# Regrouped score blocks, scaled queries and a two-part value product in a one-layer attention trunk

## The chip, the cores and the metric

The kernel runs on one core of a Trainium2 chip. The metric is the device time of one execution in microseconds (us). Five engines run side by side, each with an instruction queue of its own that it works off in order: TensorE (PE in the profile; PEld is its weight load), VectorE (DVE), ScalarE (ACT), GpSimd (POOL) and SyncE (SP, which here only issues transfers). TensorE writes to PSUM, eight banks of 512 fp32 columns; VectorE and ScalarE read it; GpSimd works in SBUF only.

## The reference, cut to what matters

One layer, 512 tokens, width 2048, sliding-window attention of 32 query heads (head dimension 64) over 4 key heads, a sink per head, a bias by distance, then a gated output product and a second gated block with an embedding. Everything is fp32.

```python
hn = x * rsqrt(mean(x*x) + eps) * norm_g
q, k, v, gate = split(hn @ w_in)                 # 2048, 256, 256, 2048 columns
scores = q.k / 8 + bias[distance]                # only 0 <= distance < 128
probs = exp(scores - m) / (sum(exp(scores - m)) + exp(sink - m))
x = x + ((probs @ v) * silu(gate)) @ w_out
g = sigmoid(rmsnorm(x) @ ple_gate)
out = rmsnorm(x + (p @ ple_proj) * g) * final_g
```

## The kernel before, in words

**Numbers.** fp32 operands are split into two rounded parts, high and low: ScalarE copies the high part (a CAST), VectorE subtracts it from the source to get the low part. A product is three matmuls (`mm3`, L117 to L122): high by high, low by high, high by low. A weight chunk of 128 x 1024 is loaded by SyncE (`Weights.load`, L99), split by ScalarE (`whi`, L106) and VectorE (`wlo`, L107), and used by eight steps of three 512-column matmuls. `Weights.get` splits two chunks ahead.

**First stage (L184 to L246).** For each of 16 slices k of the width: load a slice of x (transposed, with the norm's gain) and 768 columns of weights, split both, and multiply into PSUM: two banks of queries (`qps`, 6 matmuls of 512 columns), two of keys (`ktps`, 6 of 512), and four of values (`vps`, one per 128 tokens, 12 matmuls of 256 columns, half of each bank). Before it, 34 small matmuls (`warm_ps`, L136) run while the first loads land. The row norm 1 / rms (`rstd1`) is worked out from x on the side; it is a column per 128 tokens, and four transposes at the end of the stage (L249) and two copies (L251) spread it over the partitions as `rb`.

**Seam (L253 to L310).** `evac_q` splits a query bank into a tile of 8 groups of 64 queries, two heads side by side; keys and values are multiplied by 1 / rms, keys are laid out per key head (`make_key`), values are split (`V`), and GpSimd builds the differences of neighbouring value blocks (`diffs`, L333 and L334). The queries stay undivided; the score addition does that with `sclq`. GpSimd builds the table of the bias by distance (L299 to L310) and sends it to DRAM (`tdram`); SyncE reads back a skewed copy per pair of head pairs (`load_bias`, L359).

**Attention (L311 to L478).** 64 units: 8 sets `d` of four heads by 8 groups `g` of 64 queries. Unit i does `scores(i)`, then `turn(i-2)` and `weigh(i-3)` ahead of it, and between them seven steps (21 matmuls of 512 columns) of the projections of queries and gates, taken from a generator (`proj`). `scores` does two matmuls (L376), one per head pair, with 128 rows = 2 heads x 64 queries, over 128 keys (first two groups) or 192 keys, high and low part of the keys side by side: 256 or 384 columns. One two-bank tile takes them (`s`, one buffer: the next unit's matmuls wait until VectorE has read it). VectorE adds bias and both parts (L385 twice, with `sclq` as a per-row factor), folds the ends together (L400, since 192 keys hold 128 in the window), reduces the maximum (L402); ScalarE takes the exponential (L405); VectorE the reciprocal (L406); ScalarE scales (L408). `turn` transposes the result (L418) and splits it (L420, L421); `weigh` multiplies by V.

**Order.** The order on TensorE and SyncE is that of the program, on GpSimd too in the attention stage; the order on VectorE and ScalarE in the seam and the attention stage is set when the program is built, by a scheduler that sorts by expected readiness. [...]

**End.** After two Strassen-like products (L480 to L940) the last block of 128 rows is done in halves (`block`, L992); then a chain of one-column operations gives the last row norm (L1072 to L1077), and the four quarter rows are scaled (L1082, L906, L1083) and stored, two from SyncE's queue and two from ScalarE's (L901).

Of the kernel before, what the change touches and what calls it, by code (L numbers as in the profile page):

```python
# [11 lines left out]
F32 = mybir.dt.float32  # L12
F32R = mybir.dt.float32r
AF = mybir.ActivationFunctionType
ALU = mybir.AluOpType
# [4 lines left out]
S = 512  # L20
# [10 lines left out]
UNITS = S // HB  # L31
BUCKETS = 32
# [6 lines left out]
WARM = 34  # L39
PAD = 104  # L40
# [13 lines left out]
def trunk_kernel(ctx: ExitStack, tc: tile.TileContext, a: dict):  # L54
# [62 lines left out]
    def mm3(ps, sh, sl, mh, ml, first, last, more=False):  # L117


        nc.tensor.matmul(ps, sh, mh, start=first, stop=False, skip_group_check=more)  # L120
        nc.tensor.matmul(ps, sh, ml, start=False, stop=False, skip_group_check=more)  # L121
        nc.tensor.matmul(ps, sl, mh, start=False, stop=last, skip_group_check=more)  # L122


    sinkb = const.tile([P, PAIRS], F32, name="sinkb")
# [6 lines left out]
    ones = const.tile([P, P], mybir.dt.bfloat16, name="ones")  # L132
    nc.vector.memset(ones, 1.0)
# [10 lines left out]
    sclq = const.tile([P, UNITS], F32, name="sclq")  # L144
# [41 lines left out]
    for k in range(KC):  # L186
        wh = start_pool.tile([P, 768], F32R, tag="w0h", name=f"w0h{k}")
        wl = start_pool.tile([P, 768], F32R, tag="w0l", name=f"w0l{k}", bufs=2)
# [4 lines left out]
        cuts = [slice(512, 768), slice(0, 512)] if k == 0 else [slice(0, 768)]  # L193
        for c in cuts:
            nc.sync.dma_start(w0[:, c], a["w_first"][k][:, c])
# [10 lines left out]
        for c in cuts[-1:]:  # L206
            nc.scalar.copy(wh[:, c], w0[:, c])
            nc.vector.tensor_sub(wl[:, c], w0[:, c], wh[:, c].bitcast(F32))
# [4 lines left out]
        if f:  # L213
            for n, (sw, mx) in enumerate(((wh, h), (wl, h), (wh, l))):
                for t in range(2):
                    nc.tensor.matmul(q_ps[t], sw[:, qc[t]], mx, start=n == 0, stop=False)
        else:
            for t in range(2):
                mm3(q_ps[t], wh[:, qc[t]], wl[:, qc[t]], h, l, f, e)
# [11 lines left out]
        if k == 9:  # L231
            run(rsqrt_mean(rstd1, ssq1, D, "r1"))
            for e in range(2):
                for b in range(2):
                    nc.vector.tensor_scalar_mul(
                        sclq[HB * e : HB * e + HB].rearrange("p (n b) -> p n b", b=2)[:, :, b],
                        rstd1[HB * b : HB * b + HB], HD ** -0.5,
                    )
        if k == 10:
            for e in range(2):  # L240
                nc.sync.dma_start(sinkb[HB * e : HB * e + HB], a["sinks"][e].partition_broadcast(HB))
            nc.sync.dma_start(pn, a["ple_norm"])
        if k == 12:
            misc = quarter("misc")
            rcol = misc[:, 0].rearrange("p (t c) -> p t c", t=NB)
            nc.vector.tensor_copy(rcol, rstd1.unsqueeze(2).to_broadcast([P, NB, P]))  # L246
    W.load(3)
    for t in range(NB):
        nc.tensor.transpose(v_ps[t // 2][:, 256 + (t % 2) * P : 384 + (t % 2) * P], rcol[:, t, :], ident)  # L249
    for t in range(2):  # L250
        nc.vector.tensor_copy(rb[:, t * 256 : (t + 1) * 256], v_ps[t][:, 256:])  # L251
# [3 lines left out]
    def evac_q(c, ps):  # L255

        q = Q[c] = kvq.tile([P, UNITS, 2, HB], F32R, tag="q", name=f"q{c}", bufs=4)
        halves = slice(0, 64), slice(64, 128)
        for e in range(2):
            src = ps[halves[e]].rearrange("p (g q) -> p g q", q=HB)  # L260
            hi, lo = q[halves[e], :, e], q[halves[1 - e], :, e]
            nc.scalar.copy(hi, src)
            nc.vector.tensor_sub(lo, src, hi.bitcast(F32))

    for c in range(2):
        evac_q(c, q_ps[c])
# [26 lines left out]
    for t in range(NB):  # L293
        nc.vector.tensor_scalar_mul(heads(values[t]), heads(v_ps[t][:, :256]), rstd1[:, t : t + 1])
    split(V[0], values[0])


    relb, tvec = misc[:HEADS, 1, :BUCKETS], misc[:HEADS, 2, :TOEP]
# [25 lines left out]
    DV = apool.tile([P, NB - 1, 2, KVH * 2 * HD], F32R, name="DV")  # L324
    diffs = {}
# [26 lines left out]
    def load_bias(d):  # L352
        biases[d] = apool.tile([P, 2, P + HB], F32, tag="bias", name=f"bias{d}", bufs=2)
        for e in range(2):
            src = bass.AP(
                tensor=tdram.tensor, offset=tdram.offset + (4 * d + e) * TOEP + HB,
                ap=[[1, HB], [2 * TOEP, 2], [1, P + HB]],
            )
            nc.sync.dma_start(biases[d][HB * e : HB * e + HB], src)  # L359

    def scores(i):

        d, g = divmod(i, UNITS)
        odd = g % 2
        if g == 4 and d + 1 < TWOS:
            load_bias(d + 1)
        key = K[d // 2]

        first = max(g - 2, 0) * HB
        n = P if g < 2 else P + HB
        s_ps = spsum.tile([P, 2, S], F32, tag="w", name=f"s{i}")
        for u in range(2):
            st = Q[2 * d + u][:, g].rearrange("p e q -> p (e q)")
            nc.tensor.matmul(s_ps[:, u, : 2 * n], st, key[:, :, first : first + n], start=True, stop=True)  # L376
        t = apool.tile([P, 2, 4 + P + HB], F32, tag="t", name=f"t{i}", bufs=4)
        seen = t[:, :, 65:194] if odd else t[:, :, 0:129]
        pr = t[:, :, 65:193] if odd else t[:, :, 1:129]
        sink = 193 if odd else 0  # L380
        nc.gpsimd.tensor_copy(t[:, :, sink], sinkb[:, 2 * d : 2 * d + 2])
        bias = biases[d][:, :, ::-1]

        def add(out, in0, in1):
            nc.vector.scalar_tensor_tensor(  # L385
                out=out, in0=in0, scalar=sclq[:, g : g + 1], in1=in1, op0=ALU.mult, op1=ALU.add
            )

        if g < 2:
            if g == 0:  # L390
                nc.gpsimd.memset(t[:, :, 65:129], MASKED)
            n = HB * (g + 1)
            out = pr[:, :, :n]
            add(out, s_ps[:, :, :n], bias[:, :, 192 - n :])
            add(out, s_ps[:, :, P : P + n], out)
# [6 lines left out]
        nc.vector.tensor_reduce(sm[:, 0:2], seen, axis=AX.X, op=ALU.max, negate=True)  # L402
        for u in range(2):
            su = seen[:, u, :]
            nc.scalar.activation(su, su, AF.Exp, bias=sm[:, u : u + 1], accum_out=sm[:, 2 + u : 3 + u])  # L405
        nc.vector.reciprocal(sm[:, 4:6], sm[:, 2:4])  # L406
        for u in range(2):
            nc.scalar.mul(pr[:, u], pr[:, u], sm[:, 4 + u : 5 + u])  # L408
        T[i] = pr

    def turn(i):
# [8 lines left out]
        nc.scalar.copy(r[:, 0], pt)  # L420
        nc.vector.tensor_sub(r[:, 1], pt, r[:, 0].bitcast(F32))  # L421
# [635 lines left out]
    base, ms, rt, im, nw, yn = (const.tile([P, 1], F32, name=f"{v}_3") for v in ("base", "ms", "rt", "im", "nw", "yn"))  # L1057
# [4 lines left out]
    last = block(1, 1, "s", "o", slice(256, 512))()  # L1062
    next(last)
    run(g)
    n = done[3]
    nc.vector.tensor_reduce(base, ssq3[:, 3, : n - 1], axis=AX.X, op=ALU.add)
    nc.vector.tensor_scalar(base, base, 1.0 / D, EPS, op0=ALU.mult, op1=ALU.add)
    next(last)
# [8 lines left out]
    nc.vector.scalar_tensor_tensor(out=yn, in0=rt, scalar=im, in1=nw, op0=ALU.mult, op1=ALU.mult)  # L1077
    for j, h in ((0, 2), (1, 3)):
        if j:
            row(3, j, yn)  # L1080
        else:
            nc.vector.tensor_scalar_mul(x1[j][:, 3, :], x1[j][:, 3, :], yn)  # L1082
        nc.scalar.mul(x1[h][:, 3, :], x1[h][:, 3, :], yn)  # L1083
        store(3, j)
        store(3, h, nc.scalar)


def laid_out(i):
# [24 lines left out]
        "sinks": f(np.asarray(i["swa_sinks"])[0].reshape(PAIRS, 2).T),  # L1113
# [19 lines left out]
```

## Time and profile before

| | us |
|---|---|
| median of 3 runs (lowest, highest) | 804.79 (804.75, 805.07) |
| the profiled execution | 804.96 |
| its span, first to last instruction | 803.0 |
| TensorE busy in the span | 792.2 (99%) |
| VectorE, ScalarE, GpSimd busy | 593.0, 500.8, 111.5 |

How to read it: rows of a timeline give the start from the beginning of the span, the duration, the engine and the line, the tiles (output <- inputs), the shape and a count; a bracket at the end is idle time before the row and what ended it. Matmuls overlap, so a matmul's price is the distance from its start to the next one's, not its duration. In groups by line, the two numbers after the bar are total busy us and mean ns of one.

### The profile page before, as it was taken

What the parts mean: (1) busy time and instruction counts of PE and PEld (TensorE: products, weight loads), DVE (VectorE), ACT (ScalarE), POOL (GpSimd) and SP (SyncE); (2) the same over time, 40 slices, a digit from 0 to 9 for tenths busy, and PEclk for the clock granted to TensorE, in tenths of its full rate; (3) what the DMA queues carried; (4) which work ended last, traced back from release to release, by engine and by line L of the source; (5) the groups of instructions that cost most, each with busy time, mean ns of one, the idle gap of its engine ahead of it and who ended that gap; (6) DMA issues with size and microseconds to landing.
All of it is one profiled execution on the core that took longest, in us unless ns stands there. A gap on an engine that the chain in (4) does not pass through costs nothing.

```text
span 803.0 us, 11080 instructions
## 1 busy us (share of the span) xinstructions
PE 792.2 (99%) x3828; PEld 664.9 (83%) x3828; DVE 593.0 (74%) x967; ACT 500.8 (62%) x1038; POOL 111.5 (14%) x216
## 2 busy tenths in 40 slices
PE   9999999999999999999999999999999999999995
PEld 8888888888888888888888888888888888888884
DVE  4547786887777777777778898766646656989896
ACT  5645466676667666675666655555568656657755
POOL 0101113122121313112122200030000020210000
PEclk9999999999999999999999999999999999999998
DMA  8862587778697877868694469998512996785533
GB/s 300 312 199 94 161 266 208 224 198 237 149 249 209 206 224 194 224 172 233 169 233 122 115 213 362 322 286 243 198 53 82 373 210 200 162 227 177 194 106 105
DMA packets 45144, 164.91 MB, mean 205 GB/s; under 512 B 5904, under 2 KB 8080, under 8 KB 41248
## 3 DMA queue, kind: packets, MB, share of 16 engines
q1 hardware_dynamic: 38080, 130.07, 47.9%
q0 software_dynamic: 6720, 33.61, 22.6%
q8 instruction: 30, 0.49, 0.2%
q10 hardware_dynamic: 288, 0.52, 0.2%
q14 instruction: 26, 0.21, 0.1%
HBM read 158.36 MB, written 46.19 MB: 255 GB/s over the span
## 4 chain that ended last, share of the span: by engine, by line
PE 96%; issue 1%; DVE 1%; ACT 0%; POOL 0%; ACTq 0%; DVEq 0%; POOLq 0%
PE gps L121 7%; PE gps L122 7%; PE gps L120 7%; PE qps L121 7%; PE qps L122 7%; PE qps L120 7%; PE o L121 6%; PE o L122 6%; PE o L120 6%; PE g L122 5%; PE g L121 5%; PE g L120 5%; PE s L376 2%; PE o L454 2%; PE pt L418 2%
## 5 line engine op out<-in xcount | busy, mean ns | idle before, releaser
L563 DVE TENSOR_TENSOR blo<-braw,bhi 128x1024 fp32r<-128x1024 f32 x80 | 97.6, 1223 | 38.5 <-ACT bhi L562 38.5
L562 ACT CAST bhi<-braw 128x1024 fp32r<-128x1024 f32 x80 | 84.0, 1051 | 65.2 <-PE g L122 19.2
L122 PE MATMUL gps<-xh,wlo 128*128 128x512 f32 x256 | 100.2, 391 | 0.0
L121 PE MATMUL gps<-xl,whi 128*128 128x512 f32 x256 | 100.2, 391 | 0.0
L120 PE MATMUL gps<-xh,whi 128*128 128x512 f32 x256 | 99.9, 390 | 0.0
L107 DVE TENSOR_TENSOR wlo<-wraw,whi 128x1024 fp32r<-128x1024 f32 x60 | 73.3, 1222 | 23.0 <-ACT whi L106 20.5
L122 PE MATMUL qps<-xh,wlo 128*128 128x512 f32 x224 | 87.8, 392 | 0.0
L120 PE MATMUL o<-bhi,fho 128*128 128x512 f32 x224 | 87.7, 392 | 0.0
L121 PE MATMUL qps<-xl,whi 128*128 128x512 f32 x224 | 87.7, 391 | 0.0
L121 PE MATMUL o<-blo,fho 128*128 128x512 f32 x224 | 87.3, 390 | 0.0
L122 PE MATMUL o<-bhi,flo 128*128 128x512 f32 x224 | 87.2, 389 | 0.0
L120 PE MATMUL qps<-xh,whi 128*128 128x512 f32 x224 | 87.2, 389 | 0.0
L106 ACT CAST whi<-wraw 128x1024 fp32r<-128x1024 f32 x60 | 62.9, 1049 | 29.6 <-PE gps L121 15.3
L405 ACT ACTIVATE t<-t,sm 128x129 f32<-128x129 f32 x128 | 50.5, 396 | 44.5 <-DVE sm L402 44.4
L430 POOL TENSOR_SCALAR_AFFINE_SELECT own<-r 64x512 fp32r<-64x512 f32 (+1 forms) x48 | 34.0, 709 | 296.0 <-DVE r L421 285.6
L120 PE MATMUL g<-bhi,fhg 128*128 128x512 f32 x192 | 75.1, 391 | 0.0
L122 PE MATMUL g<-bhi,flg 128*128 128x512 f32 x192 | 74.8, 389 | 0.0
L121 PE MATMUL g<-blo,fhg 128*128 128x512 f32 x192 | 74.7, 389 | 0.0
L122 PEld LDWEIGHTS gps<-xh,wlo 128*128 128x128 f32 x256 | 48.1, 188 | 10.2
L563 DVE TENSOR_TENSOR blo<-grown,bhi 128x1024 fp32r<-128x1024 f32 x32 | 39.1, 1224 | 23.6 <-ACT bhi L562 20.4
L120 PEld LDWEIGHTS gps<-xh,whi 128*128 128x128 f32 x256 | 48.1, 188 | 9.0
L121 PEld LDWEIGHTS gps<-xl,whi 128*128 128x128 f32 x256 | 48.1, 188 | 8.9
(202 smaller groups left out, 1728.7 us busy)
## 6 DMA issues: line engine op xcount, KB each, us to landing
wraw<-in_w_gate_in SPq DMA_DIRECT2D x32, 512.0 KB, 5.7
wraw<-in_w_q SPq DMA_DIRECT2D x28, 512.0 KB, 4.7
w_out<-in_w_out POOLq DMA_DIRECT2D x24, 512.0 KB, 7.8
braw<-in_w_out SPq DMA_DIRECT2D x24, 512.0 KB, 3.5
braw<-in_ple_gate SPq DMA_DIRECT2D x24, 512.0 KB, 4.2
w_out<-in_w_out SPq DMA_DIRECT2D x16, 512.0 KB, 6.1
ple_gate<-in_ple_gate SPq DMA_DIRECT2D x16, 512.0 KB, 5.9
ple_gate<-in_ple_gate POOLq DMA_DIRECT2D x16, 512.0 KB, 7.5
```

The costliest lines, as they stand in the source:

```text
L106: nc.scalar.copy(hi, raw)
L107: nc.vector.tensor_sub(lo, raw, hi.bitcast(F32))
L120: nc.tensor.matmul(ps, sh, mh, start=first, stop=False, skip_group_check=more)
L121: nc.tensor.matmul(ps, sh, ml, start=False, stop=False, skip_group_check=more)
L122: nc.tensor.matmul(ps, sl, mh, start=False, stop=last, skip_group_check=more)
L376: nc.tensor.matmul(s_ps[:, u, : 2 * n], st, key[:, :, first : first + n], start=True, stop=True)
L405: nc.scalar.activation(su, su, AF.Exp, bias=sm[:, u : u + 1], accum_out=sm[:, 2 + u : 3 + u])
L418: nc.tensor.transpose(pt[:, u * P : (u + 1) * P], pr[:, u, :], ident)
L430: nc.gpsimd.affine_select(out=flat(own), in_=flat(r).bitcast(F32), pattern=[[0, 8], [sign, HB]], compare_op=ALU.is_ge, fill=0.0, base=-HB ...
L454: nc.tensor.matmul(out, first, r[:, low], start=low == 0, stop=own is None and low == 1)
L562: nc.scalar.copy(hi, raw)
L563: nc.vector.tensor_sub(lo, raw, hi.bitcast(F32))
```

## The change

1. A unit now covers 64 queries as two blocks of 32 queries, each of four heads (128 rows = 4 heads x 32 queries). A block needs 160 keys, not 192, and the first blocks fewer: 32, 64, 96, 128 (twice as many columns, for both parts of the keys).
2. `evac_q` multiplies the whole query bank by 1 / rms and 1 / 8 in place (one VectorE operation of 128 x 512) before the split; the score additions lose the factor `sclq`. In the first two groups the additions are made per block.
3. In the first stage the product of the values takes high x by both weight parts as one matmul of 512 columns, and low x by the high part as one of 256; the two halves of a bank are added when the values are evacuated (one more VectorE operation for each of 4 tiles).
4. `rb` comes by DRAM: GpSimd writes `rstd1` out and reads it back spread over the partitions, in slice 9. The four transposes and two copies go. `misc`, in which the bias table is built, is allocated after the seam.
5. At the start: 37 warm-up matmuls rather than 34, on a constant that exists already; slice 1 is split in two cuts. At the end: the last half block's first subtraction is issued behind the squares of the half before, the last scaling is done in smaller pieces on both engines, and three of four last stores go to SyncE's queue.

```diff
+QB = P // 4
+KEYS = P + QB
-WARM = 34
+WARM = 37
-    ones = const.tile([P, P], mybir.dt.bfloat16, name="ones")
-    nc.vector.memset(ones, 1.0)
+    ones = nc.const_aps.tensor(1.0, [P, P], mybir.dt.bfloat16)
...
-            mm3(v_ps[t][:, :256], h[:, c], l[:, c], wh[:, 256:512], wl[:, 256:512], f, e)
+            for part in "hl" if f else "lh":
+                if part == "h":
+                    nc.tensor.matmul(v_ps[t], h[:, c], both[:, :, 256:512], start=f, stop=e, skip_group_check=True)
+                else:
+                    nc.tensor.matmul(
+                        v_ps[t][:, :256], l[:, c], wh[:, 256:512], start=False, stop=False, skip_group_check=True
+                    )
...
+            rdram = tc.dram_tile([NB, P], F32, name="rdram")
+            nc.gpsimd.dma_start(rdram.rearrange("t p -> p t"), rstd1)
+            nc.gpsimd.dma_start(rb, rdram.rearrange("t p -> (t p)").partition_broadcast(P))
...
-        if k == 12:
-            misc = quarter("misc")
-            rcol = misc[:, 0].rearrange("p (t c) -> p t c", t=NB)
-            nc.vector.tensor_copy(rcol, rstd1.unsqueeze(2).to_broadcast([P, NB, P]))
     W.load(3)
-    for t in range(NB):
-        nc.tensor.transpose(v_ps[t // 2][:, 256 + (t % 2) * P : 384 + (t % 2) * P], rcol[:, t, :], ident)
-    for t in range(2):
-        nc.vector.tensor_copy(rb[:, t * 256 : (t + 1) * 256], v_ps[t][:, 256:])
+    W.get(0)
...
-        q = Q[c] = kvq.tile([P, UNITS, 2, HB], F32R, tag="q", name=f"q{c}", bufs=4)
+        d, u = divmod(c, 2)
+        if u == 0:
+            Q[d] = kvq.tile([P, S // QB, 4, QB], F32R, tag="q", name=f"q{d}", bufs=2)
+        nc.vector.scalar_tensor_tensor(out=ps, in0=ps, scalar=HD ** -0.5, in1=rb, op0=ALU.mult, op1=ALU.mult)
...
-        nc.vector.tensor_scalar_mul(heads(values[t]), heads(v_ps[t][:, :256]), rstd1[:, t : t + 1])
+        nc.vector.tensor_scalar_mul(values[t], v_ps[t][:, :256], rstd1[:, t : t + 1])
+        nc.vector.scalar_tensor_tensor(
+            out=values[t], in0=v_ps[t][:, 256:], scalar=rstd1[:, t : t + 1], in1=values[t], op0=ALU.mult, op1=ALU.add
+        )
...
-        first = max(g - 2, 0) * HB
-        n = P if g < 2 else P + HB
         s_ps = spsum.tile([P, 2, S], F32, tag="w", name=f"s{i}")
+        number = [min(2 * g + u + 1, 5) * QB for u in range(2)]
         for u in range(2):
-            st = Q[2 * d + u][:, g].rearrange("p e q -> p (e q)")
+            first, n = max(2 * g + u - 4, 0) * QB, number[u]
+            st = Q[d][:, 2 * g + u].rearrange("p h q -> p (h q)")
             nc.tensor.matmul(s_ps[:, u, : 2 * n], st, key[:, :, first : first + n], start=True, stop=True)
...
-            add(t[:, :, 1:193], s_ps[:, :, :n], bias)
-            add(t[:, :, 1:193], s_ps[:, :, n : 2 * n], t[:, :, 1:193])
-            ends = t[:, :, 1:65], t[:, :, 129:193]
-            nc.vector.tensor_max(ends[odd], ends[0], ends[1])
+            x = t[:, :, 1 : 1 + KEYS]
+            nc.vector.tensor_add(x, s_ps[:, :, :KEYS], bias.unsqueeze(1).to_broadcast([P, 2, KEYS]))
+            nc.vector.tensor_add(x, s_ps[:, :, KEYS : 2 * KEYS], x)
+            nc.vector.tensor_max(two(1, W + P, QB), t[:, :, 1 : 1 + QB], t[:, :, 1 + P : 1 + KEYS])
...
+    nc.scalar.mul(ys, rt, im)
     nc.vector.scalar_tensor_tensor(out=nw, in0=rt, scalar=im, in1=rt, op0=ALU.mult, op1=ALU.mult)
     nc.vector.tensor_scalar(nw, nw, -0.5, 1.5, op0=ALU.mult, op1=ALU.add)
-    nc.vector.scalar_tensor_tensor(out=yn, in0=rt, scalar=im, in1=nw, op0=ALU.mult, op1=ALU.mult)
+    nc.scalar.mul(yn, ys, nw)
+    scaled(xs[0])
+    store(3, 0)
+    nc.scalar.mul(xs[2], xs[2], yn)
+    store(3, 2)
+    scaled(xs[1][:, :256])
...
+    store(3, 1)
+    nc.scalar.mul(xs[3][:, :256], xs[3][:, :256], yn)
+    scaled(xs[3][:, 256:])
+    store(3, 3, nc.scalar)
```

With other tiles and other waits, the order set when the program is built differs too. In the changed program VectorE makes the low part of weight chunk 3 (`wlo`, its first use is TensorE's second projection, step 8) behind the additions and the maximum of units 0 and 1, and chunk 4's right after; in the program before, chunk 3's stands ahead of unit 0's additions and chunk 4's between them. ScalarE's high part of chunk 3 stands behind unit 0's first exponential; before, it stood ahead of all exponentials. GpSimd's copy of the sinks for unit 0, which now waits for TensorE's values of slice 13, stands ahead of the building of the bias table; before, it stood behind it.

More of the change, by code (lines that the diff above doesn't have):

```diff
@@ L205, in trunk_kernel @@
         )
-        for c in cuts[-1:]:
+        for c in cuts[1:] if k == 0 else cuts:
             nc.scalar.copy(wh[:, c], w0[:, c])
@@ L212, in trunk_kernel @@
         qc = [slice(512 + t * P, 512 + (t + 1) * P) for t in range(2)]
-        if f:
-            for n, (sw, mx) in enumerate(((wh, h), (wl, h), (wh, l))):
+        if k < 2:
+            for n, (sw, mx) in enumerate(((wh, h), (wl, h), (wh, l)) if f else ((wh, h), (wh, l), (wl, h))):
                 for t in range(2):
-                    nc.tensor.matmul(q_ps[t], sw[:, qc[t]], mx, start=n == 0, stop=False)
+                    nc.tensor.matmul(q_ps[t], sw[:, qc[t]], mx, start=f and n == 0, stop=False)
         else:
@@ L378, in scores @@
[L378 to L387, printed above, removed]
-        if g < 2:
[L390 to L395, printed above, removed]
-        else:
-            add(t[:, :, 1:193], s_ps[:, :, :n], bias)
-            add(t[:, :, 1:193], s_ps[:, :, n : 2 * n], t[:, :, 1:193])
-            ends = t[:, :, 1:65], t[:, :, 129:193]
-            nc.vector.tensor_max(ends[odd], ends[0], ends[1])
+        W = KEYS + 2
@@ new lines, in scores, with two @@
+        t = apool.tile([P, 2, W], F32, tag="t", name=f"t{i}", bufs=3)
+        at = t[:, 0, 0:1]
+        def two(of, stride, n):
+            return bass.AP(tensor=at.tensor, offset=at.offset + of, ap=[at.ap[0], [stride, 2], [1, n]])
+        late = QB if g >= 2 else 0
+        seen = [t[:, 0, 0 : P + 1], t[:, 1, 1 + late : P + 2 + late] if late else t[:, 1, 0 : P + 1]]
+        both = two(0, W + 1 + late if late else W, P + 1)
+        pr = [t[:, u, 1 + late * u : 1 + late * u + P] for u in range(2)]
@@ L407, in scores @@
         for u in range(2):
-            nc.scalar.mul(pr[:, u], pr[:, u], sm[:, 4 + u : 5 + u])
-        T[i] = pr
+            out, src = T[i][:, u], pr[u]
+            if late and (g + u) % 2:
+                out = out.rearrange("p (h k) -> p h k", h=2)[:, ::-1]
+                src = src.rearrange("p (h k) -> p h k", h=2)
+            nc.scalar.mul(out, src, sm[:, 4 + u : 5 + u])
     def turn(i):
@@ L1074, in trunk_kernel, with scaled @@
     nc.vector.reciprocal(im, ms)
+    nc.scalar.mul(ys, rt, im)
     nc.vector.scalar_tensor_tensor(out=nw, in0=rt, scalar=im, in1=rt, op0=ALU.mult, op1=ALU.mult)
     nc.vector.tensor_scalar(nw, nw, -0.5, 1.5, op0=ALU.mult, op1=ALU.add)
[L1077 to L1085, printed above, removed]
+    nc.scalar.mul(yn, ys, nw)
+    def scaled(x):
+        nc.vector.tensor_scalar(x, x, ys, nw, op0=ALU.mult, op1=ALU.mult)
+    xs = [x1[j][:, 3, :] for j in range(4)]
+    scaled(xs[0])
[3 more added lines that the diff above has]
+    scaled(xs[1][:, :256])
+    nc.vector.scalar_tensor_tensor(
+        out=xs[1][:, 256:], in0=xs[1][:, 256:], scalar=yn, in1=gain(1)[:, 256:], op0=ALU.mult, op1=ALU.mult
+    )
+    store(3, 1)
+    nc.scalar.mul(xs[3][:, :256], xs[3][:, :256], yn)
+    scaled(xs[3][:, 256:])
+    store(3, 3, nc.scalar)
 def laid_out(i):
```

76 lines of the change are left out of this document (43 added, 33 removed).

## The prediction

> **What bounds the kernel now.** I read the page first: busy shares, slices, the chain that ended last.
>
> ```profile
> span 803.0 us, 11080 instructions
> PE 792.2 (99%) x3828; PEld 664.9 (83%) x3828; DVE 593.0 (74%) x967; ACT 500.8 (62%) x1038; POOL 111.5 (14%) x216
> ...
> PEclk9999999999999999999999999999999999999998
> ...
> PE 96%; issue 1%; DVE 1%; ACT 0%; POOL 0%; ACTq 0%; DVEq 0%; POOLq 0%
> ```
>
> TensorE is busy for 99%, at full granted clock, and the chain is 96% TensorE. The table by stretches says whether anything else is near:
>
> ```profile
> core 0: us, PE busy (x) PEld busy (x) DVE busy (x) ACT busy (x) POOL busy (x), PEclk, DMA share, GB/s
> ...
> 76.20:82.10 5.90, 5.90 (x28) 4.89 (x27) 5.84 (x8) 3.39 (x6) 5.42 (x7) 1.00 0.74 260
> 82.10:88.00 5.90, 5.90 (x29) 4.90 (x27) 5.78 (x10) 3.62 (x6) 1.76 (x3) 1.00 0.00 0
> ...
> 94.70:200.00 105.30, 105.30 (x515) 88.39 (x514) 82.22 (x166) 70.21 (x190) 20.98 (x43) 1.00 0.81 232
> ```
>
> In the attention stage VectorE has 22% to spare, but from 76 to 88 us, the seam, it is full (11.62 of 11.8): there TensorE keeps going only because its next weights are already split. So the change is worth what it takes off TensorE's queue, less the waits that a fuller VectorE makes in the seam.
>
> **The score matmuls.** Rows of the chain give the price of a pair:
>
> ```profile
> 84.50 0.23 PE s L376 x2
> 94.76 0.35 PE s L376 x2
> 592.75 0.87 PE tp L802 x8
> ...
> L376 PE MATMUL s<-k,q 128*128 128x384 f32 x96 | 24.7, 338 | 0.0
> ...
> L376 PE MATMUL s<-k,q 128*128 128x256 f32 x32 | 6.4, 282 | 0.0
> ```
>
> A matmul of 256 columns costs 0.115, one of 384 costs 0.175. Per set of four heads before: 12 x 0.175 + 4 x 0.115 = 2.56. After: 12 of 320 columns at 0.145 (halfway), one of 256 at 0.115, and one each of 64, 128 and 192. No matmul of this kind under 256 columns is in the trace. Nearest row: the transposes, 128 columns, 0.87 / 8 = 0.109 each in a run of eight. I take 0.109 for each of the three (0.33): 2.18, saved 0.38 x 8 sets = **3.0 us**. Ends: at the price of columns alone (0.06 per 128) the three cost 0.165 and the saving is 4.3; were a short one to run at a quarter of the rate, as 256, 512 and 768 columns, they would cost 0.115 + 0.23 + 0.35 = 0.695 and the saving is 0.1.
>
> The Trainium skill has a figure for short ones, in "TensorE: Matmul & The Clock Gate", Back-to-back issue gap: about 81 ns for 128 columns with their weight loads. The transposes' row (109 ns) is above it; by the page the three would cost at most 0.24 and the saving would be near 3.7.
>
> **The values of the first stage.** 12 matmuls of 256 columns per slice become four of 512 and four of 256.
>
> ```profile
> 64.61 0.40 PE L120 MATMUL qps<-xh,w0h 128*128 128x512 f32 x1
> ...
> 67.36 0.28 PE L120 MATMUL vps<-w0h,xh 128*128 128x256 f32 x1
> ...
> 68.79 0.40 PE L120 MATMUL qps<-xh,w0h 128*128 128x512 f32 x1
> ```
>
> Twelve wide ones take 2.75 (0.229 each), twelve narrow ones 1.43 (0.119 each). After: 4 x (0.229 + 0.119) = 1.39; 0.04 x 16 slices = **0.7 us** saved.
>
> **The four transposes.**
>
> ```profile
> 72.85 0.28 PE L122 MATMUL vps<-w0h,xl 128*128 128x256 f32 x1
> ...
> 73.64 0.40 PE L121 MATMUL gps<-xl,whi 128*128 128x512 f32 x1
> ```
>
> From the last value matmul to the second projection matmul pass 0.79 us; without transposes 0.12 + 0.23: **0.4 us** saved. In their place 1 / rms travels by DRAM as soon as it is worked out, and is needed at 69:
>
> ```profile
> L165 DVE TENSOR_TENSOR rstd<-y_r,t_r x2: 161/161/161, 37.8 to 624.4; 128x4 f32<-128x4 f32 x2
> ```
>
> Two small transfers, one after the other, fit into 31 us even at the slowest landing that a bias load shows (10.8, quoted below), so I cost them at nothing.
>
> **What the seam gets in return.** VectorE gains two multiplications of 128 x 512, four operations on the values and two more small additions, and loses two copies.
>
> ```profile
> L488 DVE SCALAR_TENSOR_TENSOR gate<-gps,gate 128x512 f32<-128x512 f32 x16 | 10.9, 683 | 0.1
> ...
> L294 DVE TENSOR_SCALAR values<-vps,rstd 128x256 f32<-128x256 f32 x4 | 1.9, 479 | 0.1
> ...
> L251 DVE COPY rb<-vps 128x256 f32<-128x256 f32 x2 | 0.7, 415 | 0.0
> ```
>
> That is 2 x 0.68 + 4 x 0.48 - 0.83 = 2.5 us on an engine without a gap. Ahead of it, query bank 0 goes multiply, copy, subtract, copy, subtract in series (0.68 + 0.58 + 0.69 + 0.58 + 0.69 = 3.2, 3.4 with handing over) before the first projection may write it:
>
> ```profile
> 69.68 2.60 ACT L262 CAST q<-qps 64x512 fp32r<-64x512 f32 x4 [6.15 <-PE qps L122]
> 70.30 2.72 DVE L263 TENSOR_TENSOR q<-qps,q 64x512 fp32r<-64x512 f32 x4 [4.64 <-ACT q L262]
> ```
>
> Bank 0 is ready 3.29 before the value matmuls end at 72.97, or 3.25 after the change: a wait of **0.2**. The larger one is behind it. In the changed order chunk 3's low part stands behind unit 1's maximum.
>
> ```profile
> 82.59 1.23 DVE L107 TENSOR_TENSOR wlo<-wraw,whi 128x1024 fp32r<-128x1024 f32 x1
> 84.34 0.40 PE L376 MATMUL s<-k,q 128*128 128x256 f32 x2
> ...
> 89.36 0.40 PE L376 MATMUL s<-k,q 128*128 128x256 f32 x2
> 90.91 0.42 DVE L402 TENSOR_REDUCE sm<-t 128x2 f32<-128x258 f32 x1
> ```
>
> Before, VectorE ends unit 1's maximum at 91.33 with both low parts done. After: less 2 x 1.2 (both move behind it), plus 2.5, plus 0.6 for gaps in the series above, less 0.7 (earlier start): 91.3, then 1.2 for chunk 3: 92.5. TensorE is due there earlier: stage end 72.3, wait 0.2, 48 matmuls of 0.229 to unit 0 at 83.5, 5.0 to unit 1 (the two rows), one step and two matmuls more (0.23 + 5 x 0.229 = 1.4): 89.9. A wait of **2.4**, part of it ahead of unit 1, since its scores wait until unit 0's are read. Together **2.6 us**. Ends: 0 if VectorE keeps two to three us that I have not seen, 4.5 if it loses two more to GpSimd:
>
> ```profile
> L286 DVE TENSOR_TENSOR V<-values,V x4: 450/954/959, 78.3 to 80.5; 128x256 fp32r<-128x256 f32 x4
> L286 DVE TENSOR_TENSOR diffs<-diffs x2: 416/416/416, 86.8 to 88.3; 128x256 fp32r<-128x256 f32 x2
> ```
>
> The same operation takes up to 959 ns beside GpSimd's differences and 416 without. The differences move with the values, from 76 to about 81 us, closer to the units.
>
> The Trainium skill, "SBUF — State Buffer", Terms, describes a shared port pair that VectorE and GpSimd hold one at a time, the other blocked for a whole instruction. By that, both extra microseconds of the upper end would come; the two rows agree with it, and the wait would be 4.5.
>
> Behind it: chunk 4's low part follows at once and is needed 5 us later. The bias table's start moves, since GpSimd now waits for slice 13 (two slices of 4.1 before 72.3: 64.1).
>
> ```profile
> 17.78 0.69 POOL L299 DMA_DIRECT2D misc<-in_rel  x1 [16.40 <-ACT xn L230]
> ...
> 26.63 0.53 POOL L310 DMA_DIRECT2D tdram<-misc  x1 [0.31 <-POOL misc L308]
> ...
> 73.04 1.29 SPq L359 DMA_DIRECT2D bias<-tdram  x2
> ...
> DMA to landing us min/median/max: 2.8/5.0/10.8
> ```
>
> From loading the table's source to sending it pass 8.85. A bias load lands 5.0 us after its issue in the median, and I take that for the sending too. From 64.1: sent at 73.0, landed at 78.0; SyncE issues four bias loads (2.6 at 0.65 each) and then chunk 3 at 80.6. With 5.0 more to land, both are there by 86; VectorE wants the bias at 88, ScalarE chunk 3 at about 89.5. Cost nothing, margin two to three us.
>
> **The attention stage.** VectorE's additions shrink from 384 to 320 columns, about 0.12 each; the multiplication of a query bank adds 0.69 in 14 units. Load per set: 12 x 0.12 + 6 x 0.07 less 2 x 0.69, even. Cover where it is thinnest, in a unit with an evacuation:
>
> ```profile
> 166.37 0.62 DVE L385 SCALAR_TENSOR_TENSOR t<-s,sclq,t 128x384 f32<-128x384 f32 x1
> ...
> 168.38 0.51 PE L376 MATMUL s<-k,q 128*128 128x384 f32 x2
> ```
>
> The scores are read at 166.99 and the next ones come at 168.38: 1.4 us of margin, 1.0 after the change. Cost nothing.
>
> **Start and end.** Three more warm-up matmuls begin earlier, since their constant needs no VectorE; the first stage then still waits for the split weights: nothing. At the end:
>
> ```profile
> 796.32 0.22 DVE L1077 SCALAR_TENSOR_TENSOR yn<-rt,im,nw 128x1 f32<-128x1 f32 x1
> 796.57 0.72 ACT L1083 ACTIVATE x<-x,yn 128x512 f32<-128x512 f32 x1 [0.88 <-DVE yn L1077]
> ...
> 797.75 0.72 ACT L1083 ACTIVATE x<-x,yn 128x512 f32<-128x512 f32 x1 [0.45 <-ACT x L1083]
> 798.50 0.34 ACTq L901 DMA_DIRECT2D out<-x  x1
> ```
>
> The last quarter row is now halved between two engines and no longer stands behind ScalarE's store: ready near 797.8 rather than 798.47. I take **0.6 us** (ends 0 and 0.7).
>
> **Sum.** -3.0 - 0.7 - 0.4 - 0.6 + 2.6 = -2.1. The profiled execution took 804.96 (span 803.0 and 1.96 around it), 0.17 above the median of 804.79, so 802.9 beside it and **802.7** as a median.
>
> **Rivals.** All beside the median.
> - *Seam without the wait, or short matmuls at the price of columns*: -4.7, or -3.4: 800.1 to 801.4. For it: VectorE's handovers are estimated; against it: the order is fixed and the engine full.
> - *Short matmuls at a quarter of the rate*: 2.9 of the 3.0 go: 805.6. Against it: the 128-column transposes do not cost 0.23. For it: nothing narrower than 256 columns but transposes is in the trace.
> - *The bias table or chunk 3 lands late*: past 88 us each us is one more of waiting; 3 us late gives 805.7.
> - *VectorE falls behind at the query evacuations* (the other side): multiply, copy, subtract, copy, subtract passes between two in-order engines five times. If that costs a unit over 1.0 us more than the 0.69, TensorE waits for the rest before the next scores (one buffer). At 0.5 over, 14 x 0.5 = 7: 809.7. Against it: 22% idle; for it: this is where idle does not help, since the queue is in order.
>
> **How the numbers follow.** Forecast 0.42, first rival 0.22, quarter rate 0.16, late table 0.07, evacuations 0.13. Bound of no change: 0.2%, 1.6 us, about what a measurement can tell (803.2 to 806.4). The forecast's own spread (801.5 to 804.5) is faster in six of ten. Faster: 0.25 + 0.22 = 0.47. Same: 0.17 + 0.11 + 0.035, 0.315. Slower: 0.05 + 0.035 + 0.13 = 0.215. The range 800.2 to 807.0 leaves out the evacuations and a little of both ends.
>
> **What would show it.** Score pairs at 0.29 and the sets' first pairs near 0.22 (0.35 or more: quarter rate); first stage's end at 72.3; chunk 3's low part ending at 92 to 93 with a gap in TensorE's starts ahead of it; bias loads issued by 78.5; no gap ahead of scores after 100 us; last store issued near 797.9. Wrong it is if those gaps recur in the evacuating units, or if short matmuls miss 0.109 widely.

## The result, and the profile after

The change made the kernel slower: 809.85 us, median of 6 runs (808.68 to 810.93), against 804.93 (804.61 to 805.10, 6 runs); ratio 1.006, 95% interval 1.0049 to 1.0071. Forecast was 802.7, range 800.2 to 807.0. The profiled execution took 808.68, its span 806.5; it is the shortest of the six (the other spans are 807.2 to 808.8). Its page:

```profile
span 806.5 us, 11059 instructions
PE 790.6 (98%) x3763; PEld 657.9 (82%) x3763; DVE 588.3 (73%) x1014; ACT 499.6 (62%) x1041; POOL 114.3 (14%) x234
```

TensorE has less to do than before and the span is longer: it waits. The view of the waits (us in total, times, longest) says for whom; before, the same view shows none longer than 0.3 behind the first stage.

```profile
PE o L123 <- DVE blo L584: 1.3, 3, 0.5
PE gps L122 <- ACT whi L108: 0.9, 1, 0.9
PE g L123 <- DVE blo L584: 0.9, 1, 0.9
PE s L387 <- DVE t L408: 0.9, 1, 0.9
PE o L477 <- ACT own L458: 0.9, 2, 0.5
...
PE gps L124 <- DVE wlo L109: 0.5, 1, 0.5
```

Three places: the seam (`whi`, `wlo`, `s` behind L408), the attention stage's end (`own`), and the low parts of weights in the two stages behind it (`blo`), which the change doesn't touch. How much each costs is read from where the same instruction starts in the traces of the kernels told of below (us from the span's start; the last line is the span):

| | before | after | sink | both | order3 | first_last |
|---|---|---|---|---|---|---|
| unit 0's scores | 84.34 | 82.97 | 83.11 | 83.04 | 82.89 | 82.62 |
| set 1's first scores | 128.76 | 130.13 | 131.33 | 128.71 | 126.83 | 127.07 |
| set 7's first scores | 401.92 | 402.10 | 400.45 | 397.83 | 395.94 | 399.93 |
| last projection matmul | 458.58 | 459.00 | 456.59 | 453.97 | 452.09 | 456.60 |
| first matmul of `g` | 617.02 | 619.56 | 615.25 | 612.92 | 610.73 | 615.21 |
| last matmul | 793.34 | 797.22 | 793.01 | 789.99 | 788.40 | 792.52 |
| span | 803.0 | 806.5 | 802.3 | 799.3 | 797.7 | 802.0 |

From before to after: -1.4 by unit 0, +2.7 in set 0 (the seam), -1.2 in sets 1 to 6, +0.2 to the end of the projections, +2.1 in the output product, +1.3 in the second gated block, -0.4 at the end: 3.5 longer. The seam's rows of after:

```profile
87.74 0.39 PE L124 MATMUL gps<-xh,wlo 128*128 128x512 f32 x1
89.03 0.47 PE L387 MATMUL s<-k,q 128*128 128x192 f32 x2 [0.90 <-DVE t L408]
...
89.80 0.40 PE L124 MATMUL gps<-xh,wlo 128*128 128x512 f32 x1
...
90.06 1.03 ACT L108 CAST whi<-wraw 128x1024 fp32r<-128x1024 f32 x1
...
91.12 1.23 DVE L109 TENSOR_TENSOR wlo<-wraw,whi 128x1024 fp32r<-128x1024 f32 x1 [0.24 <-ACT whi L108]
...
91.14 0.50 PE L122 MATMUL gps<-xh,whi 128*128 128x512 f32 x1 [0.94 <-ACT whi L108]
91.48 0.40 PE L123 MATMUL gps<-xl,whi 128*128 128x512 f32 x1
92.40 0.50 PE L124 MATMUL gps<-xh,wlo 128*128 128x512 f32 x1 [0.53 <-DVE wlo L109]
```

The distances 1.29, 1.34 and 0.92, where 0.23 is usual, make 2.9 us. The waits at unit 1's scores and at chunk 3's low part, which ends at 92.35, were forecast at this place; the 1.1 at its high part was not.

**The wait that nobody had counted** is seen in VectorE's waits of the attention stage (95 to 445 us), of before and then of after:

```profile
DVE sm L402 <- POOL t L381: 3.1, 5, 0.7
```

```profile
DVE t L411 <- POOL t L399: 13.2, 20, 0.9
```

Before, only the maximum (`sm`) waits for GpSimd's copy of the sinks, and it comes three operations behind the first addition. After, the first addition (L411) waits for it, and that copy stands behind the selection of the own block, which waits for `turn`. The last unit shows it, GpSimd and then VectorE of after, and VectorE and TensorE:

```profile
443.42 0.66 POOL L451 TENSOR_SCALAR_AFFINE_SELECT own<-r 128x512 fp32r<-128x512 f32 x1 [3.43 <-DVE r L442]
444.02 0.19 POOL L399 COPY t<-sinkb 128x2 f32<-128x2 f32 x1
```

```profile
442.92 0.42 DVE L442 TENSOR_TENSOR r<-pt,r 128x256 fp32r<-128x256 f32 x1
444.25 0.49 DVE L411 TENSOR_TENSOR t<-s,bias 128x320 f32<-128x320 f32 x1 [0.90 <-POOL t L399]
...
453.55 0.39 PE L477 MATMUL o<-own,DV 128*128 128x256 f32 x1 [0.41 <-ACT own L458]
```

The addition starts 0.90 late, and ScalarE's exponential and the first splits of the output weights follow about 1 us later than before. The own block then holds TensorE up, and VectorE goes into the output product 1 us behind.

In sets 1 to 6 most of the loss is too short for the view of the waits. Six times VectorE's second addition (L412) is late behind the evacuation of a query bank, and the next scores start 0.14 to 0.15 us after its end, since they have one buffer; twice TensorE waits for the own block's copy. Of after, and then of the kernel with the sinks apart (told of below), at the same unit:

```profile
169.13 0.49 DVE L412 TENSOR_TENSOR t<-s,t 128x320 f32<-128x320 f32 x1
169.30 0.28 PE L477 MATMUL o<-own,DV 128*128 128x256 f32 x1
...
169.76 0.53 PE L387 MATMUL s<-k,q 128*128 128x320 f32 x2 [0.19 <-DVE t L412]
```

```profile
169.26 0.49 DVE L413 TENSOR_TENSOR t<-s,t 128x320 f32<-128x320 f32 x1
...
170.41 0.28 PE L478 MATMUL o<-own,DV 128*128 128x256 f32 x1
170.53 0.46 PE L387 MATMUL s<-k,q 128*128 128x320 f32 x2
```

No data demand the wait: the copy writes columns 0 and 323 of a tile whose additions write 1 to 160 and 163 to 322. But it is written as one operand of two columns 323 apart, and in the built program the first additions of units 2 and up of each set wait for TensorE and GpSimd both. In units 0 and 1 of a set, where the two columns lie 162 apart (a row of the tile), and in the program before, where they lie a row of its tile apart, GpSimd is not among their waits.

### The profile page after: what moved, and what is told of

Same layout as the page of the kernel before. It is cut to its first block, busy times and chain, and to the rows that moved or that the text cites. A ratio compares the mean times of both kernels' runs of the same rounds, so it can differ in the third digit from the quotient of the medians.

```text
span 806.5 us, 11059 instructions
## 1 busy us (share of the span) xinstructions
PE 790.6 (98%) x3763; PEld 657.9 (82%) x3763; DVE 588.3 (73%) x1014; ACT 499.6 (62%) x1041; POOL 114.3 (14%) x234
```

## The experiments

Each label is one kernel; its time stands beside the program before on the same chip.

**The changed kernel again.**

> The changed kernel once more, nothing edited, for a second profile. Its first profile (span 806.5) has TensorE waiting in three places that the program before does not have: 2.9 us in the seam (87.7 to 92.7), 0.65 at 452.7 and 2.1 at 467.8, 482.1 and 485.6 behind low parts of the output weights, and 1.3 at 754.8 behind a load that landed 4.9 us after its issue, where the same load of the program before took 3.2. If these come from the order of the queues, all of the first two groups stand there again within 0.3 us. If they are chance landings of transfers, the group at 467 to 486 goes or moves, and the time is nearer to 806. The wait at 754.8 I expect elsewhere or gone, as chance. Time by the first theory 809 to 811, about 5 above the program before.

808.95 (808.57 to 809.69); before 805.11; ratio 1.0049 (1.0037 to 1.0062). The seam's three waits, `own`, and the first `blo` wait (now at 470.2) stand again to within 0.1; of the other two in the output product neither does. In the first profile they lay behind a row of x that landed 8.1 us after its issue and had VectorE stand for 2.82, so I take those two for chance. The wait at the end, which I took for chance, came back: 0.92 ahead of 756.24. New is a slow stretch behind the seam. Rows of the table by stretches (us, PE busy, PEld, DVE, ACT, POOL, granted clock, DMA share, GB/s) of this run, and then of the first profile of after:

```profile
89.12:92.53 3.41, 1.93 (x8) 1.02 (x8) 3.04 (x9) 2.78 (x7) 0.00 (x0) 1.00 0.88 243
92.53:95.94 3.41, 3.41 (x8) 2.73 (x9) 1.39 (x2) 2.04 (x8) 0.26 (x1) 0.50 1.23 287
95.94:99.35 3.41, 3.41 (x18) 2.79 (x18) 0.71 (x2) 1.08 (x2) 0.00 (x0) 1.00 0.80 279
```

```profile
89.69:93.10 3.41, 1.94 (x8) 0.97 (x7) 3.03 (x8) 3.41 (x10) 0.00 (x0) 1.00 0.89 247
93.10:96.51 3.41, 3.41 (x18) 2.80 (x17) 0.74 (x2) 1.39 (x6) 0.26 (x1) 1.00 1.11 280
```

Same waits, but here the granted clock is 0.50 for 3.41 us behind them: 8 matmuls rather than 18, some 1.5 us lost (set 1 begins at 131.82, not 130.13). The Trainium skill, "TensorE: Matmul & The Clock Gate", Part 1: The HAM clock gate, says that the clock is halved after a window of about 3.4 us without activity, and that the window runs freely. The halved clock and the 3.41 us agree with that, and so does the place of the drop: by the clock's record in this trace the granted clock rose to 1.00 at 3.78 and fell at 92.53, 26 times 3.41 us later. That TensorE was busy 1.93 of the 3.41 us ahead of the drop does not fit a window that has to be idle throughout. Nor does busy time alone tell the two runs apart (1.93 with a drop, 1.94 without); what decides is open.

**The sinks apart.** In the changed kernel:

```diff
-        nc.gpsimd.tensor_copy(two(0, W + W - 1 if late else W, 1), sinkb[...])
+        nc.gpsimd.tensor_copy(t[:, 0, 0:1], sinkb[:, d : d + 1])
+        nc.gpsimd.tensor_copy(t[:, 1, W - 1 : W] if late else t[:, 1, 0:1], sinkb[:, d : d + 1])
```

> The changed kernel with GpSimd's copy of the sinks made as two one-column copies, so that it no longer counts as touching the columns that VectorE's first addition writes. In the changed kernel VectorE waited 13.2 us in 20 units for that copy, which stands behind the selection of the own block in GpSimd's queue; before, it never did ahead of an addition. Theory of the sink: the last unit's addition, maximum, exponential and with them the first split of the output weights come 1.0 us earlier, so the wait at 452.7 (0.65) and those at 467 to 486 (2.1) go, and some 0.5 to 1 of the waits in the attention stage: 2 to 4 us below the changed kernel, 806 to 808. Rival of the transfers: VectorE's idle time in the attention stage is cover enough, the late waits come from landings, and the time stays at 809 to 811 though VectorE no longer waits for GpSimd. The seam's 2.9 stays by both.

803.54 (802.22 to 804.70, 11 runs); before 805.11; ratio 0.998 (0.9971 to 0.9989). That is 5.4 us below the changed kernel, more than either theory gave, and it turns the change from slower to a little faster. The addition's wait for GpSimd is gone from the view of VectorE's waits. Sets 1 to 6 take 269.1 rather than 272.0 us, the output product (last projection matmul to first of `g`) 158.7 rather than 160.6 (159.2 in the second profile of the changed kernel), and TensorE no longer waits for `own` or for `blo` at 453 to 486. The slow stretch is in this trace too (granted clock 0.50 from 91.46 to 94.87, about 1.1 us of set 0). What TensorE still waits for:

```profile
PE g L123 <- DVE blo L585: 1.0, 1, 1.0
PE gps L122 <- ACT whi L108: 0.9, 1, 0.9
PE s L387 <- DVE t L409: 0.9, 1, 0.9
```

**The same wait given to the program before.**

```diff
-        nc.gpsimd.tensor_copy(t[:, :, sink], sinkb[:, 2 * d : 2 * d + 2])
+        wide = slice(sink - odd, sink - odd + 2)
+        nc.gpsimd.tensor_copy(t[:, :, wide], sinkb[:, 2 * d : 2 * d + 2].unsqueeze(2).to_broadcast([P, 2, 2]))
```

> The program before, with one thing changed: GpSimd's copy of the sinks writes the sink's column and the key column next to it, which VectorE's first addition then overwrites. So the addition has to wait for GpSimd, as it does in the changed kernel; the arithmetic is the same. Theory of the sink: VectorE waits for that copy in about 20 units, the last unit's exponentials and the first splits of the output weights come about 1 us later, and the program before gets slower by 2 to 4 us (807 to 809), with waits at the last own block and at the output weights like those of the changed kernel. Rival: what made the changed kernel slow is its own order and tiles, and this copy alone costs the program before under 0.8 us.

811.18 (810.98 to 813.36); before 805.16; ratio 1.0078 (1.0064 to 1.0091). This one wait makes the program before 6 us slower, more than expected, and in another place than expected: not in the output product, but ahead of scores.

```profile
PE s L376 <- DVE t L386: 3.9, 7, 0.9
...
PE o L457 <- ACT own L438: 0.8, 1, 0.8
```

The wait is also larger here than in the changed kernel (VectorE waits 19.4 us in 33 units, not 13.2 in 20), and the program before has less room there: its additions are 0.62 long where those of the change are 0.49. That the addition's wait for GpSimd costs 5 to 6 us is shown from both sides.

**Value blocks later.** The differences are built at unit 2 rather than 0, and the splits of value blocks 1 to 3 and of the differences are queued behind the split of chunk 4 (`W.four`):

```diff
-        if i == 0:
-            for n in range(1, NB):
-                make_diff(n)
-        if 1 <= i < NB:
-            split(V[i], values[i])
-            spread_diff(i)
+        if 2 <= i < NB + 2:
+            with tc.issue_after(W.four[0].ins), tc.issue_after(W.four[1].ins):
+                if i == 2:
+                    for n in range(1, NB):
+                        make_diff(n)
+                else:
+                    split(V[i - 2], values[i - 2])
+                    spread_diff(i - 2)
```

> The changed kernel with the differences and the splits of value blocks 1 to 3 (three times V, three times diffs: some 3.6 us of VectorE in the seam, five of the six slowed by GpSimd) queued behind the split of weight chunk 4, two units later. Theory of the full VectorE: units 0 and 1 and chunk 3's low part come over 3 us earlier, the 2.9 us of the seam shrink to under 0.5, and the time falls by 2.4 to 2.9 to about 807. Rival of the order: chunk 3's high part still stands behind unit 0's first exponential, and the wait is a matter of that order alone: then 1 us or more of it stays. Rival of a wait that is only moved: the differences are needed at unit 5, and TensorE waits there instead.

808.82 (808.46 to 809.18); before 805.11: only 0.1 below the changed kernel. In its trace the three seam waits have become one, of 1.6, as the rival of the order allowed (1 us or more stays): 3.4 us less for VectorE (0.79, 0.96 and 0.41 for the values, three times 0.41 for the differences, so two of the six were slowed and not five), and only 1.3 of 2.9 gone. The profiled span (805.4) is 1.3 below that of the changed kernel's second profile (806.7), the median time only 0.1. In the profiled execution late waits (0.64 at 501, 1.29 at 755) take back some of the gain; the other four spans are 806.4 to 806.9, and where they lost the rest no trace shows.

**Both edits.**

> Both edits, the sinks apart and the value splits behind chunk 4. If the two losses are separate, the gains add up: 5 to 6.5 us below the changed kernel, 803.5 to 805, level with the program before or a little faster, which leaves of the change its gains on TensorE (first stage 1.2, scores 0.28 per set of heads, tail 0.4) less what the late stages still lose. If the late waits are chance landings, it stays at 806 to 808.

801.88 (801.55 to 801.91); before 805.11; ratio 0.9959 (0.9946 to 0.9971): 7.1 below the changed kernel, more than the 5 to 6.5 expected. On top of the sinks the later values gain 1.7, and the times lie within 0.4 us of each other; the slow stretch behind the seam isn't there in its trace. What is left of the seam's wait:

```profile
86.09 0.42 DVE L419 TENSOR_REDUCE sm<-t 128x2 f32<-128x258 f32 x1
88.47 0.46 DVE L410 TENSOR_TENSOR t<-s,bias 128x96 f32<-128x96 f32 x2 [1.96 <-PE s L390]
...
89.73 1.22 DVE L108 TENSOR_TENSOR wlo<-wraw,whi 128x1024 fp32r<-128x1024 f32 x1
...
91.00 0.50 PE L125 MATMUL gps<-xh,wlo 128*128 128x512 f32 x1 [1.42 <-DVE wlo L108]
```

VectorE stands idle for 1.96 us for unit 1's scores with chunk 3's low part queued behind them. It is no longer full; it is in the wrong order.

**The order mended too.** Unit 0's exponentials are queued behind chunk 3's high part, unit 1's additions behind its low part (`chunks.three`):

```diff
+                with tc.issue_after(chunks.three[1].ins) if i == 1 else nullcontext():
                     nc.vector.tensor_add(t[:, u, 1 : 1 + n], s_ps[:, u, :n], bias[:, KEYS - n :])
...
+            with tc.issue_after(chunks.three[0].ins) if i == 0 else nullcontext():
                 nc.scalar.activation(su, su, AF.Exp, ...)
```

> The kernel with both edits, and the order in the seam mended: unit 0's exponentials are queued behind the high part of chunk 3 on ScalarE, and unit 1's additions behind its low part on VectorE. With both edits VectorE stood idle for 1.96 us (to 88.47) with that low part queued behind unit 1's additions, and TensorE then waited 1.6 us for it. Theory of the order: with the idle stretch used for the low part, the seam's wait goes altogether, 1.4 to 1.7 us: 800.2 to 800.5 if both edits give 801.9. Rival of the full engine: the wait comes back at unit 1's or unit 2's scores, and less than 0.8 is gained.

800.30 (799.78 to 801.13); before 805.16; ratio 0.9939 (0.9926 to 0.9951). TensorE no longer waits in the seam, and 1.6 us are gained, as the theory of the order says. So of the seam's 2.9, about 1.3 went with VectorE's load and 1.6 with its order, mended in this sequence; the order alone, with the values where they were, was not run. Behind the first stage one wait is left:

```profile
PE g L126 <- DVE blo L592: 0.9, 1, 0.9
```

**The late wait.** It stands in every profile of the changed kernel and of the four kernels made from it so far, and not in the program before. It goes back to one load of 512 KB, here in before and then in after:

```profile
L555 SPq DMA_DIRECT2D braw<-in_ple_gate x1: 327/327/327, 738.0 to 738.0; - x1
...
DMA to landing us min/median/max: 3.2/3.2/3.2
```

```profile
L576 SPq DMA_DIRECT2D braw<-in_ple_gate x1: 328/328/328, 740.5 to 740.5; - x1
...
DMA to landing us min/median/max: 4.9/4.9/4.9
```

In the queues' view of each microsecond, a packet of the queue named instruction (16 KB) lies at 743 in after, and in before at 724 and 754:

```profile
q8 instruction: 1, 0.02, 6.0%
```

6.0% of 16 engines for 1 us is one transfer engine for about 1 us. There are 29 such packets in the run, for 2 x 3763 instructions of TensorE: one per 130 matmuls. The change issues 65 matmuls fewer, half of that, and so moves the packet by half a period, onto this load. The test has 64 small matmuls more at the start, on the kernel with both edits:

```diff
+    for _ in range(64):
+        nc.tensor.matmul(warm_ps[:16, :16], ones[:, :16], ones[:, :16], start=True, stop=True)
     for _ in range(WARM):
```

> The kernel with both edits, and 64 matmuls of 16 columns ahead of the warm-up ones, whose results are not used: they move TensorE's place in its instruction stream by half a block of its instruction transfers (one 16 KB packet of the queue named instruction per 128 matmuls, about 29 us). In all five profiles of the changed kernel and its variants such a packet falls on the load issued 15.6 us ahead of the late wait at 749 to 756, which lands 4.6 to 5.1 us after its issue; in the program before the packet falls 13 us later, and the load lands after 3.2. Theory of the instruction packet: it moves by about 14.5 us away from that load, the load lands after 3.2 to 3.6, and the wait (0.5 us here, 0.9 to 1.5 in the others) goes. Rival: the load is late for another reason, and lands after 4.6 to 5.1 again. The time itself says less: the small matmuls cost 0 to 4 us at the start (0.03 to 0.06 each, partly beside the wait for the first weights).

801.42 (800.70 to 802.24), before 805.16. The packet moved from 734 to 752, the load landed after 3.2, and the wait is gone from TensorE's view. The second gated block takes 176.3 us from first to last matmul, as in the program before (177.1 with both edits, 177.7 in after). The start lost 0.65.

**Parts 3, 4 and 5 alone,** on the program before, with scores and queries as they were:

> The program before with parts 3, 4 and 5 of the change alone (the values by both parts of the weights, 1 / rms by DRAM, start and end); score blocks, queries and the attention stage as before. From the traces so far: the first projection starts 1.2 to 1.3 us earlier (71.9 to 72.1 rather than 73.3), the end gains 0.4, and VectorE gets 1.1 us more in the seam (four operations of 0.48 less two copies of 0.42) where the whole change gives it 2.5, so the seam's wait is 0 to 1. TensorE issues 65 matmuls fewer ahead of the late stages, as many as in the whole change; by the theory of the instruction packet the packet falls on the same load, which lands after 4.6 to 5.1, and TensorE waits about 1.1 us at 750 to 756 although nothing of these stages is changed: 803.9 to 805.2 in all. By the rival, in which the late wait belongs to the new attention stage, there is no such wait and the time is 802.8 to 804.1.

804.87 (803.91 to 805.36, 11 runs), before 805.02; ratio 0.9997 (0.9988 to 1.0006). No wait in the seam; unit 0's scores 1.7 earlier than before, the end 0.2 earlier from the last matmul on (9.5 us rather than 9.7); the profiled execution is the shortest of the eleven. The late wait is there (0.5 in the view, 0.7 by the distance), with a packet at 738, though nothing of that stage or of attention is changed: it belongs to the count of matmuls, not to the new scores. Here the three parts are worth about nothing together.

**The whole, with another warm-up:** the mended kernel with 80 small and 21 of the 37 large warm-up matmuls.

> The kernel with sinks apart, values late and the seam's order mended (800.3), and its warm-up as 80 matmuls of 16 columns (0.026 each by the trace) and 21 of 128 instead of 37 of 128: as long, but 64 matmuls more, so that TensorE's instruction packet leaves the late load. Theory of the packet: the load lands after 3.2 to 3.6, the wait of 1.05 at 747 goes, and the time is 799.0 to 799.5, the start being as before. Rival: the packet falls on another load that is as urgent, or the warm-up of mostly small matmuls leaves the clock lower for the first ones; 800 to 801.

799.84 (799.61 to 801.62); before 805.02; ratio 0.9938 (0.9925 to 0.9952): the same as without it, so the 0.8 to 1.3 us that were expected did not come. The late wait is gone, as the theory says, but in the profiled execution (801.44) unit 0's scores come 1.0 later, and TensorE waits 1.0 at 496 behind a load of the output weights that landed 7.9 us after its issue, at 494.0, beside two rows of x. The nearest packet lies at 497, so it isn't the packet; why that load was late is open. The mended kernel, with or without this warm-up, is the fastest, 0.6% below the program before.

## Why the prediction was wrong

- **The step that failed: "Cost nothing" in the attention stage.** I weighed VectorE's durations there and not its waits, though the change turns the sinks' copy into an operand with another stride, and the built program's waits name GpSimd at every first addition from unit 2 on. The text ahead of the prediction follows this very copy for unit 0, and not for the units behind it. Cost: 5.4 us in the runs (808.95 to 803.54). The table shows 2.9 of it in sets 1 to 6 (272.0 to 269.1 us); 0.8 more lies between set 7's first scores and the last projection matmul, at `own`, and 0.5 to 1.9 in the output product.
- **The rival of the evacuations** has the right time (809.7) by another cause, and that it fits so well is luck. The place was seen rightly: in the changed kernel the six late scores of these sets start 1.9 to 2.4 us behind the start of a query bank's last subtraction. But with the sinks apart the multiplication of the query banks costs no wait there, so the order of five steps was not the matter.
- **Late stages: nothing was costed.** A change in TensorE's count of instructions moved one instruction packet by some 14 us against a load with no room (2.7 us behind its issue in after, 16.9 in before): 0.8 to 1.4 us of the second gated block by the table.
- **The scores, -3.0.** Right, once the wait is gone. Added up over sets 1 to 6, from each score matmul's start to the next matmul's, the scores take 15.50 us before and 13.23 with the sinks apart: 0.38 per set, as forecast. In the changed kernel they take 13.73, or 0.30 per set, late starts among them. A pair of matmuls of 320 columns costs 0.30 (forecast 0.29), the pair of 64 and 128 columns 0.18 (forecast 0.22): short matmuls show no quarter rate. Rows of after and, the last two, of the kernel with the sinks apart:

```profile
187.11 0.46 PE L387 MATMUL s<-k,q 128*128 128x320 f32 x2
187.41 0.39 PE L122 MATMUL gps<-xh,whi 128*128 128x512 f32 x1
```

```profile
221.03 0.34 PE L387 MATMUL s<-k,q 128*128 128x64 f32 x2
221.21 0.45 PE L122 MATMUL gps<-xh,whi 128*128 128x512 f32 x1
```

Sets 1 to 6 together gain more: 269.1 rather than 273.2, 0.67 per set. By the same sums the other 0.3 lies in the projections' matmuls (230.60 to 229.81), the products with V (15.99 to 15.28) and with the own block (4.58 to 4.32); why these lie closer is open.
- **First stage, -1.1.** 1.3: the second projection matmul starts at 72.30, before at 73.64. The wait of 0.2 at bank 0 is there (71.55 to 71.96 where 0.23 is usual).
- **The seam, +2.6.** 2.9 in the three places, where the prediction has 2.4 (the 2.6 holds the 0.2 at bank 0; by its own figures, 92.5 less 89.9, it is 2.6). Chunk 3's low part ended at 92.35, as forecast. Not foretold: that the high part, costed at nothing, is waited for as well (1.1 of the 2.9; it starts at 90.06, behind unit 0's first exponential), and the slow clock behind the seam in some runs, 1.1 to 1.5 more. The bias table was no danger; its loads landed 1.9 us after their issue at the latest, and were issued from 70.4.
- **The end, -0.6.** 0.4 (from the last matmul to the end of the span 9.3 rather than 9.7).

Summed with what was measured, the steps that I had give -3.0 - 1.3 + 2.9 - 0.4 = -1.8; the span with the sinks apart is 0.7 shorter than before (802.3 and 803.0). That the two are so close is partly luck: that trace also has the slow stretch (1.1) and the late load (1.4) against it, and the 1.8 of the other matmuls in sets 1 to 6 for it.

## What to carry to other kernels

When a diff changes how an operand is addressed, read the built program's waits on both sides of it: a copy of two columns cost more here (5.4 us) than all the savings of the forecast together (4.7). A stage in which every engine has time to spare is not free of waits, since queues are in order and a small operation on a slow queue passes its delay on. And a wait in a stage that the change doesn't touch may still come from it, by the count of instructions ahead.

## What the runs showed of the hardware

- One 16 KB packet of instructions per some 130 matmuls shares the transfer engines with the loads; the 512 KB load ahead of the late wait lands 4.3 to 5.2 us after its issue where it meets one, and 3.2 where it doesn't (seven traces with, four without). The Trainium skill, "DMA: Bandwidth & Descriptors", Queues, rings and completion order, says that each transfer engine takes turns between its queues packet by packet; the rows do not speak against it, but the delay is 1.0 to 2.0 us and the packet shown takes 1; what makes up the rest isn't shown.
- A matmul of 16 columns by 16 costs 0.026 us at the start (64 of them from 0.85 to 2.53):

```profile
0.85 1.75 PE L138 MATMUL warm_ps<-const-bfloat16-1.0 128*16 128x16 bf16 x64 [0.85 <-PEq L1162]
2.53 3.36 PE L140 MATMUL warm_ps<-const-bfloat16-1.0 128*128 128x128 bf16 x37
```

- Behind a stretch of 3.41 us in which TensorE was busy 1.93, the granted clock was 0.50 for 3.41 us (8 matmuls rather than 18); behind one with 1.94 in another run it stayed at 1.00.
